# Rows of pairs 304 columns wide, and a drawn layout of weight places and product order for every five tiles

## The chip, the cores and the metric

The kernel runs on one core of one Trainium2 chip. What is compared is the device time of one execution in microseconds, as the median of several runs. Times of parts come from one profiled execution.

## The reference

Two layers of a bidirectional hybrid encoder over 16 meta tokens and 256 tokens (L = 272 rows, D = 2048), in float32. Per layer:

```
proj = h @ w_in                       # 2048 -> 6176 columns: GLA q, k, v, gate, decay, attention q, k, v
y    = [gla(q, k, v, gate, decay) | neighbourhood_attention(q, k, v)]
h    = layer_norm(alpha * h + y @ w_out)
h    = layer_norm(alpha * h + relu(h @ w_ff1)**2 @ w_ff2)     # 2048 -> 8192 -> 2048
```

The gated linear attention runs in both directions in chunks, the neighbourhood attention over a 4 x 64 grid with a relative bias. The meta rows are dropped from the output. Nearly all of the arithmetic is the four weight products.

## The kernel before

**Three products for one.** Each float32 operand is held as a high part rounded to float32r and a low part, the remainder. A product of a weight block w and an activation block x is the sum of high x high (`h`), high x low (`l`: the same weight block against the low activations) and low x high (`w`: the low weights against the high activations).

**Activations.** They lie transposed, 16 blocks of 128 features (32 for the MLP's inner layer, `y0` to `y15` and `u16` to `u31`). A block is a pair: one tile of shape 128 x 2 x PITCH, high row and low row beside each other (`pair`, L306). PITCH is 288 float32 columns, so the low row starts 288 columns after the high one, and one pair takes 2304 bytes of a partition. In the last layer the pairs of `y` and `u`, and the pairs of `x` after its first norm, are dense: their 256 + 256 columns follow each other with no gap (`Pair`, L45).

**Weights.** They come in tiles of 128 x 1024 (eight blocks of 128 x 128), 768 of them, 512 KB each, through SyncE's queue into `raw` (L189). ScalarE rounds a tile into `wh` (L212), VectorE subtracts to get `wl` (L213). `raw`, `wh` and `wl` have three buffers each, and `weights` (L175) makes each tile one ahead of the one in use. Where the eight blocks lie within a buffer of WIDE = 1280 columns is told by three numbers, the place of the first, the step from an even block to the odd one after it, and the step from pair to pair (`blocks`, L196, `HIGHS` and `LOWS`, L42 and L43). Most tiles of the first layer have the high blocks at (0, 128, 256), one run of 1024 columns, and the low ones at (0, 144, 320).

**Products by m.** `by_m` (L276) accumulates one output block of 128 features over all tiles of its weights in one PSUM bank. `eight` (L233) issues the products of a tile, in an order written as a string (`TURNS`, L44): `hlhlww` four times, 24 products of n columns, where n is 272 (layer one, and the parts of layer two that need the meta rows), 274 or 258 (two more columns carry the norm's gain and bias through the product, while the norm itself is still being computed) or 256. Where only the 256 tokens are needed (most of layer two), `once` is set: `hw` eight times, 16 products, in which `h` reads the high and the low row together, 512 columns, and `w` 256. In the attention part of layer two these 512 columns are read from a pair with a gap, as two runs of 256.

**Products by k.** `by_k` (L258) accumulates four (at the very start eight) output blocks at once, for the stages whose activations become ready one after another. Its order is its own (L273), in the same sense of `h`, `l` and `w`.

**Other work.** GLA, attention and norms are generators; `pump` (L125) advances them between tiles, so that their instructions stand in the queues of the engines between those of the products. TensorE does its part of them in between (L584 to L667 GLA, L723 to L789 attention, L910 the norms' means).

Of the kernel before, what the change touches and what calls it, by code (L numbers as in the profile page):

```python
# [2 lines left out]

# [11 lines left out]
P = 128  # L15
# [11 lines left out]
WB = 1024  # L27
# [9 lines left out]
WARM = 14  # L37
MEET = 2
PAD = 40
PITCH = 288  # L40
WIDE = 1280
HIGHS = {True: 24, False: 0}  # L42
LOWS = {True: (8, P + 32, 2 * P + 64), False: (0, P + 16, 2 * P + 64)}  # L43
TURNS = {True: "hwhwhwhwhwhwhwhw", False: "hlhlwwhlhlwwhlhlwwhlhlww"}  # L44


# [11 lines left out]
class Trunk:  # L58
    def __init__(self, ctx, tc, ins, out):
        self.ctx, self.tc, self.nc = ctx, tc, tc.nc  # L60
        self.i, self.out = ins, out
        self.bg, self.fg, self.credit, self.fcredit = deque(), deque(), 0, 0
        self.wants, self.due, self.late = {}, None, 0
        self.x = [None] * DC
        self.stream, self.ready = self.order(), deque()
        pool = lambda name, **k: ctx.enter_context(tc.tile_pool(name=name, **k))
        self.cp = pool("const", bufs=1)
        self.xp = pool("xhl", bufs=1)
        self.yp = pool("yhl", bufs=1)
        self.wp = pool("wst", bufs=3)  # L70
        self.jp = pool("jn", bufs=1)
        self.pm = pool("pm", bufs=4, space=PSUM)
        self.pb = pool("pb", bufs=4, space=PSUM)
# [80 lines left out]
    def order(self):  # L154

        i, first = self.i, [(), (WB // 2, WB)]
        for l in range(DEPTH):
            last = l + 1 == DEPTH
            na = [last and c % 3 == 0 for c in range(24)]
            groups = [(i["win"][l, g], [last and g in (3, 4, 5)] * 4 if g < 6 else na[4 * g - 24:4 * g - 20]) for g in range(12)]  # L160
            groups += [(i["wout"][l, g], [last and g > 0] * 4) for g in range(4)]
            for half in range(2):
                groups += [(i["wff1"][l, 8 * half + g], [last and (half > 0 or g > 2)] * 4) for g in range(8)]
                groups += [(i["wff2"][l, half, g], [last] * 4) for g in range(4)]
            if l == 0:
                for t in range(groups[0][0].shape[0]):
                    for w, _ in groups[:2]:
                        yield w[t], first.pop(0) if first else (WB,), False
                groups = groups[2:]
            for w, once in groups:  # L170
                n = w.shape[0]
                for t in range(n):
                    yield w[t], (WB,), once[4 * t // n]

    def weights(self):  # L175

        while len(self.ready) < 2:
            self.ready.append(self.made(*next(self.stream, (None, (), False))))
        return self.ready.popleft()

    def made(self, ap, ends, once):
        if ap is None:
            return None
        nc = self.nc
        raw = self.wp.tile([P, WB], F32, name="raw", tag="raw")
        wh, wl = (self.wp.tile([P, WIDE], F32R, name=nm, tag=nm) for nm in ("wh", "wl"))
        wh, wl = self.blocks(wh, HIGHS[once], P, 2 * P), self.blocks(wl, *LOWS[once])
        for c in map(slice, (0,) + ends, ends):
            nc.sync.dma_start(raw[:, c], ap[:, c])  # L189
            self.halves(raw[:, c], wh, wl, slice(c.start // P, c.stop // P))  # L190
        if not ends:
            self.head(ap, raw, wh, wl)
        return wh, wl
# [21 lines left out]
    def head(self, ap, raw, wh, wl):  # L215

        nc, q = self.nc, WB // 4
        both = self.xr.tile([P, 2, q + L], F32, name="head", tag="head", bufs=1)
        self.x[:2] = [self.pair(self.xp, "x", c) for c in range(2)]
        for c in range(2):  # L220
            nc.sync.dma_start(both[:, c], self.i["head"][:, c])
        nc.sync.dma_start(raw[:, 2 * q:], ap[:, 2 * q:])
        for c in range(2):
            at = slice(2 * c, 2 * c + 2)
            h, lo = (t[:, :L] for t in self.x[c])
            acts = lambda: self.split(both[:, c, q:], h, lo)
            weights = lambda: self.halves(both[:, c, :q], wh, wl, at)
            for f in (weights, acts) if c else (acts, weights):
                f()
        for at in (slice(4, 6), slice(6, 8)):  # L230
            self.halves(raw[:, at.start * P:at.stop * P], wh, wl, at)

    def eight(self, ps, wh, wl, x, n, first, last, once):  # L233

        mm = self.nc.tensor.matmul
        seen = dict.fromkeys("hlw", 0)
        for i, kind in enumerate(TURNS[once]):  # L240
            j = seen[kind]
            seen[kind] += 1
            w, v, o = wl if kind == "w" else wh, x[j], ps[:, :n]
            rhs = v[kind == "l"][:, :n]
            if once:
                rhs, o = (v.once, ps) if kind == "h" else (v[0][:, :T], ps[:, T:])
            mm(o, lhsT=self.block(w, j), rhs=rhs, start=first and not i, stop=last and i == len(TURNS[once]) - 1)  # L247

    def whole(self, parts):

# [53 lines left out]
    def pair(self, pool, name, c):  # L304
        both = pool.tile([P, 2, PITCH], F32R, name=f"{name}{c}", tag=f"{name}{c}", bufs=1)
        return Pair(both, dense=name in ("y", "u") and not self.full)  # L306
# [94 lines left out]
    def load_gates(self):  # L401

        place = lambda c: self.yp.tile([P, 2, PITCH], F32, name=f"gw{c}", tag=f"y{c}", bufs=1).rearrange("p a c -> p (a c)")[:, :512]
        *self.wup, self.wlr = (place(c) for c in (8, 9, 10))
# [563 lines left out]
    def reuse(self, name, c, dtype):  # L968

        t = self.xp.tile([P, 2, PITCH], dtype, name=f"{name}{c}", tag=f"x{c}", bufs=1)  # L970
        return t.rearrange("p a c -> p (a c)")[:, :512]
# [237 lines left out]
```

## Time and profile before

| | |
|---|---|
| median of 3 runs | 2337.14 us (2336.44 to 2337.54) |
| profiled execution | 2336.72 us, span of its instructions 2334.9 us |
| TensorE busy | 2326.3 us, 18180 matmuls |
| weight loads of TensorE busy | 2216.0 us |
| VectorE busy | 1527.4 us |
| ScalarE busy | 1211.8 us |
| granted TensorE clock, mean | 0.999 |
| read from HBM | 414.03 MB, 178 GB/s over the span |

Matmuls overlap each other in the records, and so do weight loads and matmuls: the duration of one matmul is longer than the distance between two starts. For the pace of a stage its length is divided by the number of its products.

### The profile page before, as it was taken

Reading aid. Unit: us, or ns where it says so; the run is one execution under the profiler, and the core shown is the slowest. Engines: PE = TensorE matmul, PEld = TensorE weight load, DVE = VectorE, ACT = ScalarE, POOL = GpSimd, SP = SyncE. Lnnn points to the kernel's source line nnn. Section 1 sums busy time; section 2 is a strip of 40 time slices with the busy share of each in tenths; the row PEclk is TensorE's granted clock in tenths of the full one; section 3 lists DMA queues with packets and bytes.
Section 4 is the critical chain, followed back from the end, with each engine's and each line's share of the span. In section 5 each row is a group of like instructions: output and inputs, shape, how many; then the busy total and the mean of one; then the engine's idle time right before and its main releaser. Section 6 shows DMA issues by size and latency. Waiting matters only on the chain.

```text
span 2334.9 us, 44618 instructions
## 1 busy us (share of the span) xinstructions
PE 2326.3 (100%) x18180; PEld 2216.0 (95%) x18180; DVE 1527.4 (65%) x2432; ACT 1211.8 (52%) x2100; POOL 129.4 (6%) x200
## 2 busy tenths in 40 slices
PE   9999999999999999999999999999999999999998
PEld 9999999999999999999999899989988888888888
DVE  5588777775544455546576887778766555666655
ACT  5666664564433344444456666655654334445443
POOL 0021110110000000000020111100100000000000
PEclk9999999999999999999999999999999999999999
DMA  8555545566666666665555555556666666667664
GB/s 264 154 163 154 152 140 178 173 179 181 179 182 178 180 179 181 181 181 177 178 183 168 172 163 158 162 158 189 191 191 193 193 190 191 193 193 221 190 191 151
DMA packets 118301, 419.02 MB, mean 179 GB/s; under 512 B 13512, under 2 KB 14024, under 8 KB 118096
## 3 DMA queue, kind: packets, MB, share of 16 engines
q1 hardware_dynamic: 117808, 415.65, 59.4%
q8 instruction: 142, 2.33, 0.4%
q14 instruction: 63, 0.52, 0.1%
q10 hardware_dynamic: 288, 0.52, 0.1%
HBM read 414.03 MB, written 2.10 MB: 178 GB/s over the span
## 4 chain that ended last, share of the span: by engine, by line
PE 98%; DVE 1%; issue 0%; ACT 0%; DVEq 0%; ACTq 0%
PE mm L247 86%; PE mm L273 6%; PE bg L273 1%; PE bg L784 1%; PE mm L723 1%; PE bg L584 1%; DVE wl L213 0%; PE bg L430 0%; PE mm L749 0%; DVE acc L1012 0%; PE mm L473 0%; PE bg L635 0%; PE bg L910 0%; PE bg L665 0%; PE bg L639 0%
## 5 line engine op out<-in xcount | busy, mean ns | idle before, releaser
L213 DVE TENSOR_TENSOR wl<-raw,wh 128x1024 fp32r<-128x1024 f32 (+1 forms) x770 | 942.9, 1225 | 637.8 <-ACT wh L212 631.8
L212 ACT CAST wh<-raw 128x1024 fp32r<-128x1024 f32 (+1 forms) x770 | 804.5, 1046 | 889.1 <-PE mm L247 703.0
L247 PE MATMUL mm<-x,wh 128*128 128x272 f32 (+3 forms) x5376 | 1094.3, 309 | 0.0
L247 PEld LDWEIGHTS mm<-x,wh 128*128 128x128 f32 x5376 | 803.7, 188 | 48.1 <-PE mm L723 0.6
L247 PE MATMUL mm<-x,wl 128*128 128x272 f32 (+3 forms) x3264 | 752.7, 283 | 0.0
L247 PEld LDWEIGHTS mm<-x,wl 128*128 128x128 f32 x3264 | 547.5, 188 | 0.0
L247 PE MATMUL mm<-y,wh 128*128 128x272 f32 (+2 forms) x2128 | 472.9, 319 | 0.0
L247 PEld LDWEIGHTS mm<-y,wh 128*128 128x128 f32 x2128 | 328.6, 188 | 26.9
L247 PE MATMUL mm<-u,wh 128*128 128x272 f32 (+2 forms) x1552 | 343.7, 318 | 0.0
L247 PE MATMUL mm<-y,wl 128*128 128x272 f32 (+1 forms) x1408 | 337.9, 282 | 0.7 <-DVE wl L213 0.7
L247 PEld LDWEIGHTS mm<-u,wh 128*128 128x128 f32 x1552 | 239.4, 188 | 19.5
L247 PE MATMUL mm<-u,wl 128*128 128x272 f32 (+1 forms) x1024 | 245.6, 282 | 0.0
L247 PEld LDWEIGHTS mm<-y,wl 128*128 128x128 f32 x1408 | 241.7, 188 | 1.4 <-DVE wl L213 1.1
L247 PEld LDWEIGHTS mm<-u,wl 128*128 128x128 f32 x1024 | 175.6, 188 | 0.0
L273 PE MATMUL mm<-x,wh 128*128 128x272 f32 (+1 forms) x512 | 83.8, 287 | 0.0
L273 PEld LDWEIGHTS mm<-x,wh 128*128 128x128 f32 x512 | 71.7, 191 | 0.0
L1000 POOL TENSOR_SCALAR acc<-acc,vec 128x272 f32<-128x272 f32 (+1 forms) x24 | 41.9, 1751 | 273.3 <-DVE acc L1012 155.3
L561 ACT COPY U<-S 128x272 f32<-128x272 f32 (+1 forms) x104 | 40.7, 429 | 23.2 <-DVE S L570 20.5
L273 PE MATMUL mm<-x,wl 128*128 128x272 f32 (+1 forms) x256 | 52.1, 286 | 0.5 <-DVE wl L213 0.5
L872 DVE TENSOR_TENSOR acc<-acc,mm 128x256 f32<-128x256 f32 (+1 forms) x71 | 30.3, 426 | 29.6 <-PE mm L247 29.1
L570 DVE TENSOR_TENSOR S<-S,dec 128x272 f32<-128x272 f32 (+1 forms) x112 | 46.3, 443 | 3.5 <-ACT U L561 2.5
L295 ACT CAST u<-ft 128x272 fp32r<-128x272 f32 (+1 forms) x64 | 26.2, 410 | 41.8 <-DVE ft L828 41.7
(265 smaller groups left out, 1647.5 us busy)
## 6 DMA issues: line engine op xcount, KB each, us to landing
raw<-in_wff SPq DMA_DIRECT2D x512, 512.0 KB, 3.8
raw<-in_win SPq DMA_DIRECT2D x190, 512.0 KB, 3.7
raw<-in_wout SPq DMA_DIRECT2D x64, 512.0 KB, 3.7
nb<-in_nab SPq DMA_DIRECT2D x16, 352.0 KB, 4.4
xraw<-in_xT SPq DMA_DIRECT2D x7, 272.0 KB, 5.9
out<-out SPq DMA_DIRECT2D x5, 256.0 KB, 3.1
brow<-in_norm SPq DMA_DIRECT2D x4, 256.0 KB, 4.5
gw<-in_wup SPq DMA_DIRECT2D x4, 196.0 KB
```

Source lines behind the costliest of these rows:

```text
L212: self.nc.scalar.copy(h, r)
L213: self.wl = self.nc.vector.tensor_tensor(lo, r, h.bitcast(F32), ALU.subtract).ins
L247: mm(o, lhsT=self.block(w, j), rhs=rhs, start=first and not i, stop=last and i == len(TURNS[once]) - 1)
L273: self.nc.tensor.matmul(ps[g + m][:, :n], lhsT=self.block(parts[p][0], 4 * j + m if first else 2 * m + j), rhs=acts[k + j][parts[p][1]][:, ...
L295: self.nc.scalar.copy(hi, src)
L561: nc.scalar.copy(U[:, lv % 4, j, :w].rearrange("p (n t h) -> p n t h", t=2, h=hb), bass.AP(S.tensor, S.offset + 2 * j * L, [S.ap[0], [2 * ...
L570: tt(o, o, totals(lv, odd, w), ALU.mult)
L584: nc.tensor.matmul(ps[b * 32:b * 32 + 32, o:o + w], lhsT=k[:, c:c + 32], rhs=q[:, r:r + w], start=True, stop=True)
L723: nc.tensor.matmul(ps[hh][:, t * NKEY:t * NKEY + NKEY], lhsT=q[hs, NM + t * P:NM + t * P + P], rhs=k[hs, t, :], start=True, stop=True)
L784: nc.tensor.matmul(po[t][hs, :P], lhsT=v2[ts, hs] if rest else v1[:, t, hs], rhs=p2[ts, hh, :] if rest else p1[:, 2 * hh + t, :], start=re ...
L872: tt(a, a, part, ALU.add)
L1000: nc.gpsimd.tensor_scalar(a, a, gain, bias, ALU.mult, ALU.add)
```

## The change

Two constants grow: PITCH from 288 to 304, so that a pair takes 2432 bytes and the low row starts 304 columns after the high one, and WIDE from 1280 to 1344 columns. A weight tile now has a kind instead of a flag:

- `once`: the dense short tiles, with places and order as before;
- `two`: the short tiles of layer two whose moving rows are read in two runs, with places of their own (before they had those of `once`);
- `all2` and `own2`: the tiles of 274 columns, and of 258, with places of their own (before: those of the tiles of 272);
- `all`: all else. Every five consecutive tiles of this kind draw, from a generator with a fixed seed, the first place and the step to the odd block for the high and for the low blocks (each 0 to 56 columns in steps of 8 beyond its least value; the step from pair to pair is 320 columns for both), and one of two orders of the 24 products, `hlhlww` four times or `hlw` eight times. The first two tiles of the program, which come in pieces, keep the old places. The order is used by `eight` only; `by_k` keeps its own. 86 layouts are drawn for 430 tiles: 376 by m of 272 columns, 38 by k of 272 and 16 by k of 256.

The same products are computed with the same weights; sums within a tile are added in another order where `hlw` is drawn.

```diff
-PITCH = 288
-WIDE = 1280
-HIGHS = {True: 24, False: 0}
-LOWS = {True: (8, P + 32, 2 * P + 64), False: (0, P + 16, 2 * P + 64)}
+PITCH = 304
+WIDE = 1344
+HIGHS = {"once": (24, P, 2 * P), "two": (0, P, 2 * P), "all": (0, P, 2 * P), "all2": (0, P, 2 * P), "own2": (0, P + 48, 2 * P + 64)}
+LOWS = {"once": (8, P + 32, 2 * P + 64), "two": (16, P + 16, 2 * P + 64), "all": (0, P + 16, 2 * P + 64),
+        "all2": (0, P + 48, 2 * P + 64), "own2": (0, P + 32, 2 * P + 64)}
+ORDERS = "hlhlwwhlhlwwhlhlwwhlhlww", "hlwhlwhlwhlwhlwhlwhlwhlw"
...
     def weights(self):
 
         while len(self.ready) < 2:
-            self.ready.append(self.made(*next(self.stream, (None, (), False))))
+            self.ready.append(self.made(*next(self.stream, (None, (), None))))
+        self.turn = self.turns.popleft()
         return self.ready.popleft()
 
-    def made(self, ap, ends, once):
+    def draw(self):
+
+        if self.drawn % 5 == 0:
+            r = lambda: 8 * self.dice.randrange(8)
+            self.places = (r(), P + r(), 2 * P + 64), (r(), P + r(), 2 * P + 64), ORDERS[self.dice.randrange(2)]
+        self.drawn += 1
+        return self.places
+
+    def made(self, ap, ends, kind):
...
-        wh, wl = self.blocks(wh, HIGHS[once], P, 2 * P), self.blocks(wl, *LOWS[once])
+        high, low, turn = self.draw() if kind == "all" and ends == (WB,) else (HIGHS[kind], LOWS[kind], TURNS[False])
+        self.turns.append(turn)
+        wh, wl = self.blocks(wh, *high), self.blocks(wl, *low)
...
-        for i, kind in enumerate(TURNS[once]):
+        turn = TURNS[True] if once else self.turn
+        for i, kind in enumerate(turn):
```

More of the change, by code (lines that the diff above doesn't have):

```diff
@@ L2 @@
 from contextlib import ExitStack
+from random import Random
 import concourse.bass as bass
@@ L64, in __init__ @@
         self.x = [None] * DC
-        self.stream, self.ready = self.order(), deque()
+        self.stream, self.ready, self.turns, self.drawn, self.dice = self.order(), deque(), deque(), 0, Random(5)
         pool = lambda name, **k: ctx.enter_context(tc.tile_pool(name=name, **k))
@@ L158, in order @@
             last = l + 1 == DEPTH
-            na = [last and c % 3 == 0 for c in range(24)]
-            groups = [(i["win"][l, g], [last and g in (3, 4, 5)] * 4 if g < 6 else na[4 * g - 24:4 * g - 20]) for g in range(12)]
-            groups += [(i["wout"][l, g], [last and g > 0] * 4) for g in range(4)]
+            kind = lambda short, name: name if last and short else "all"
+            na = [kind(c % 3 == 0, "two") for c in range(24)]
+            groups = [(i["win"][l, g], [kind(g in (3, 4, 5), "two")] * 4 if g < 6 else na[4 * g - 24:4 * g - 20]) for g in range(12)]
+            if last:
+                groups[0] = groups[0][0], ["all2"] * 4
+            groups += [(i["wout"][l, g], [kind(g > 0, "once")] * 4) for g in range(4)]
             for half in range(2):
-                groups += [(i["wff1"][l, 8 * half + g], [last and (half > 0 or g > 2)] * 4) for g in range(8)]
-                groups += [(i["wff2"][l, half, g], [last] * 4) for g in range(4)]
+                groups += [(i["wff1"][l, 8 * half + g], [kind(half > 0 or g > 2, "once") if half or g > 1 else ("all2", "own2")[last]] * 4)
+                           for g in range(8)]
+                groups += [(i["wff2"][l, half, g], [kind(True, "once")] * 4) for g in range(4)]
             if l == 0:
@@ L167, in order @@
                     for w, _ in groups[:2]:
-                        yield w[t], first.pop(0) if first else (WB,), False
+                        yield w[t], first.pop(0) if first else (WB,), "all"
                 groups = groups[2:]
-            for w, once in groups:
+            for w, kinds in groups:
                 n = w.shape[0]
                 for t in range(n):
-                    yield w[t], (WB,), once[4 * t // n]
+                    yield w[t], (WB,), kinds[4 * t // n]
     def weights(self):
         while len(self.ready) < 2:
-            self.ready.append(self.made(*next(self.stream, (None, (), False))))
+            self.ready.append(self.made(*next(self.stream, (None, (), None))))
+        self.turn = self.turns.popleft()
         return self.ready.popleft()
-    def made(self, ap, ends, once):
+    def draw(self):
[5 more added lines that the diff above has]
+    def made(self, ap, ends, kind):
         if ap is None:
+            self.turns.append(None)
             return None
@@ L246, in eight @@
                 rhs, o = (v.once, ps) if kind == "h" else (v[0][:, :T], ps[:, T:])
-            mm(o, lhsT=self.block(w, j), rhs=rhs, start=first and not i, stop=last and i == len(TURNS[once]) - 1)
+            mm(o, lhsT=self.block(w, j), rhs=rhs, start=first and not i, stop=last and i == len(turn) - 1)
     def whole(self, parts):
```

## The prediction

> **What bounds the kernel now.** I read the page first (parts 1, 2 and 4), then the waits of TensorE, then TensorE's groups by shape, then windows cut to single stages, and last the timeline of a few tiles.
>
> ```profile
> span 2334.9 us, 44618 instructions
> PE 2326.3 (100%) x18180; PEld 2216.0 (95%) x18180; DVE 1527.4 (65%) x2432; ACT 1211.8 (52%) x2100; POOL 129.4 (6%) x200
> PEclk9999999999999999999999999999999999999999
> ...
> PE 98%; DVE 1%; issue 0%; ACT 0%; DVEq 0%; ACTq 0%
> ```
> ```profile
> PE mm L247 <- DVE wl L213: 0.7, 1, 0.7
> PE mm L273 <- DVE wl L213: 0.5, 1, 0.5
> ```
>
> TensorE is busy for 2326.3 of 2334.9 us, at full clock in every slice, the chain that ends last is 98% TensorE, and its products by m and by k wait 1.2 us in all for weights. So neither loads nor splits set the time. What sets it is how many ns apart the products start. A busy matmul row does not show that, since one of 286 ns overlaps the next; a stage's length divided by its products does. The groups by shape give the counts:
>
> ```profile
> L247 PE MATMUL mm<-x,wh 128*128 128x272 f32 x3584 | 588.5, 286 | 0.0
> L247 PE MATMUL mm<-x,wh 128*128 128x512 f32 x1152 | 400.2, 392 | 0.0
> L247 PE MATMUL mm<-x,wl 128*128 128x272 f32 x1792 | 364.9, 285 | 0.0
> L247 PE MATMUL mm<-x,wl 128*128 128x256 f32 x1152 | 321.8, 279 | 0.0
> L247 PE MATMUL mm<-y,wh 128*128 128x272 f32 x1408 | 229.9, 285 | 0.0
> L247 PE MATMUL mm<-u,wh 128*128 128x272 f32 x1024 | 167.0, 285 | 0.0
> L247 PE MATMUL mm<-y,wl 128*128 128x272 f32 x704 | 143.2, 285 | 0.0
> L247 PE MATMUL mm<-u,wl 128*128 128x272 f32 x512 | 104.2, 284 | 0.0
> ```
>
> Products by m of 272 columns: 3584+1792+1408+1024+704+512 = 9024, which is 376 tiles of 24. From 512 against 256 columns a column costs (392-279)/256 = 0.44 ns. The windows hold whole stages and show products by m alone (length, TensorE busy, number):
>
> ```profile
> 445.50:488.06 42.56, 42.55 (x336) 1.00 0.57 173
> 1620.18:1660.87 40.69, 40.68 (x336) 1.00 0.59 181
> 816.64:1004.37 187.73, 187.73 (x1538) 1.00 0.62 180
> ...
> 1284.64:1307.40 22.76, 22.75 (x128) 1.00 0.64 189
> 1969.39:2145.18 175.79, 175.79 (x1026) 1.00 0.65 192
> ```
> and the products by k of 256 columns:
> ```profile
> 1660.87:1683.70 22.83, 22.83 (x192) 1.00 0.63 186
> ```
>
> They are, in order: tiles of 274 columns, of 258 columns, 64 tiles of 272 columns (1536 products; two more hang over from before), eight short tiles (512 and 256 by turns) whose pair is read in two runs, and 64 short tiles whose pair is dense (1024 products). Starts are 42.56/336 = 126.7, 40.69/336 = 121.1, 187.73/1536 = 122.2, 22.76/128 = 177.8 and 175.79/1024 = 171.7 ns apart, and 22.83/192 = 118.9 by k. In all six TensorE never stops, yet the width doesn't explain them. Brought to 272 columns at 0.44 ns each, 274 gives 125.8, 258 gives 127.3, and 256 gives 126.0: all slower than the 272 itself, whose weights lie at the same places. The two kinds of short tile have the same weights at the same places and the same columns, and differ by 6.1 ns a product only in how the moving rows lie. So the distance between starts depends on how the two reads of a product meet, and 272 columns over rows of 288 meet them well.
>
> The timeline where a stage of 272 columns begins (first start of each six products; line engine group) shows it within one set of addresses:
>
> ```profile
> 488.06 0.66 PE L273 MATMUL mm<-x,wh 128*128 128x272 f32 x4
> ...
> 488.81 0.67 PE L273 MATMUL mm<-x,wh 128*128 128x272 f32 x4
> ...
> 489.57 0.66 PE L273 MATMUL mm<-x,wh 128*128 128x272 f32 x4
> ...
> 490.31 0.65 PE L273 MATMUL mm<-x,wh 128*128 128x272 f32 x4
> ...
> 491.04 0.65 PE L273 MATMUL mm<-x,wh 128*128 128x272 f32 x4
> ```
>
> Three sixes take 2.25 us (125.0 ns a product), then 0.73 a six (122): the stream opens slow and settles into a faster beat. A layout whose beat is no better than the opening would stay at 125.
>
> **The change, part by part.** No matmul, DMA, cast or split is added or taken away; addresses and, in about half of the tiles, the order within a tile change.
>
> *Drawn layouts.* They reach the 376 tiles by m of 272 columns, 38 of 40 tiles by k of that width, and 16 tiles by k of 256: 430 tiles, 86 draws. Each draw moves four starts by 0 to 56 columns in steps of 8, and picks `hlhlww` or `hlw`. Before shows one layout, so I bound the mean of 86 by the nearest rows: below by 122.2, the settled beat, above by 127.3. The five values at 272 columns (127.3, 126.0, 125.8, 125.0, 122.2) have a mean of 125.3; I take 125.2, that is +3.0 ns, and 124.0 to 126.4 for the mean of many draws. There are 9024 + 38x24 = 9936 such products: 9936 x 3.0 = +29.8 us, all on the path, since TensorE has no idle time to give. What is already unsettled can't be lost again: an opening costs 2.25 - 3x0.733 = 0.05 us, and with some fifty openings (an estimate: sixteen head pairs and eight GLA heads, each cutting in two or three times) that is 2.5 us to take off. +27.3. The 256-wide tiles by k are at 126.0 for 272 already: 0.
>
> *Fixed places of the 274s, the 258s and the two-run tiles.* 24 tiles of 274 (576 products), 16 of 258 (384) and 40 short tiles read in two runs (640) get places of their own. If all reached the best beat of their width (274 at 122.2+0.9, 258 at 122.2-6.2, two runs at the dense 171.7) they gave back 576x3.6 + 384x5.1 + 640x6.1 = 2.1+2.0+3.9 = 8.0 us; if none, 0. I take half, -4.0.
>
> *Rows of 304.* Dense pairs keep their places for the weights, but a pair takes 2432 bytes instead of 2304, so in steps of 256 bytes (the 64 columns that the draws span) every second pair now starts half a step off. The some 250 dense tiles, by the code about 4000 products, stand at 171.7; the two-run row 177.8 is the other end, and below them I see room for little, as 343.4 ns for 768 columns is 0.447 a column, the lowest here. I take +0.2 ns, +0.8 us, and -1 to +3 ns for the range.
>
> *Casts and splits.* The high part, one run of 1024 for most tiles, is written in eight runs of 128; the low part is so already.
>
> ```profile
> L213 DVE TENSOR_TENSOR wl<-raw,wh 128x1024 fp32r<-128x1024 f32 x766 | 940.7, 1229 | 636.7 <-ACT wh L212 630.8 <-PE mm L247 0.7 <-PE bg L910 0.5
> L212 ACT CAST wh<-raw 128x1024 fp32r<-128x1024 f32 x766 | 802.6, 1048 | 887.9 <-PE mm L247 703.0 <-issue 91.2 <-PE mm L273 35.8
> ```
> ```profile
> 300.00:500.00 200.00, 160.19 (x314) 1.00 0.55 164
> ```
>
> A tile lasts 24x122.2 ns = 2.93 us and its cast and split 1.05+1.23 us on two engines, made a tile ahead, and both wait for TensorE (703.0 us) and for each other (630.8). `hlw` asks for the low part two products, 0.25 us, earlier. VectorE is fullest at 300 to 500 us (last row), 80%. That cover hides it: 0, and 1 us in the range. The scheduler shifts some dozens of small instructions of the GLA stage on VectorE and ScalarE: 0, at 1 us either way.
>
> Sum: 27.3 - 4.0 + 0.8 = +24.1 on the profiled execution's 2336.72 us (1.8 over its span), 2360.8; the median of the runs stands 0.4 above that execution, so 2361.
>
> A rule of the Trainium skill speaks against all of this. "TensorE: Matmul & The Clock Gate", Step-by-step, says that the array reads moving rows and weights over two independent ports, and that "Loading the next tile's weights doesn't steal SBUF read bandwidth from the running matmul." By it no place would matter and the drawn tiles would cost 0; the trace disagrees, with 171.7 and 177.8 ns for the same widths and weights and 125.0 and 122 at the same addresses, though it can't say whether weights or the moving rows' own start is at fault.
>
> **The rivals.**
>
> *Places don't matter (no effect).* The beat might belong to the width alone (272 is 17 times 16, the other two are not). For it: one width settles everywhere at 122.2, whatever the buffer. Against: the two short kinds, and 256, a rounder number, at 126.0. Then 9936 x 0 and no fixed kind gains: 2337.
>
> *The draws are better than the places before (faster).* If rows of 304 bring a better beat to most layouts, every drawn product and the fixed kinds gain. It turns at a mean of 122.5 ns (0.3 ns x 9936 = the 3 us that the fixed kinds give). Price: at the lowest cost per column seen, 0.447x272 = 121.6 ns, it is -0.6x9936 = -6.0 and -8.0: 2323. Against it: all 86 draws would have to beat the best layout that the trace shows. By the skill's figure for an undisturbed stream (same page, "Back-to-back issue gap": N/2.4 + 2.5 ns) 272 columns would take 115.8 as an estimate, and this rival would reach 2337 - 9936x6.4/1000 = 2273; no row here comes near that.
>
> *The dense short tiles lose their beat too (slower still).* Half way to the two-run row is +3 ns on 4000 products: +12 us, 2373. For it: their moving rows shift and their weights don't. Against: in a dense tile the low blocks already lie at two different places (8 and 168 columns) against rows of one, and the pace is still the best per column here.
>
> *Weights come late.* If the eight-run write took ScalarE and VectorE a third longer (0.35 and 0.4 us), the crowded 300 to 500 us would need 160 + 68x0.4 = 187 of 200 us and the chain would pass to VectorE in places: +5 us, 2366. Against: the low part is written in eight runs already, and its 1229 ns is VectorE's cost of two inputs.
>
> **How the numbers follow.** Forecast 0.70, dense tiles 0.12, late weights 0.06, no effect 0.05, faster 0.07. The forecast's own ends: mean 124.0 gives 9936x1.8 = 17.9 - 2.5 - 8.0 = +7.4, less 2 for dense and scheduling, 2342; mean 126.4 gives 41.7 - 2.5 + 3 = +42, 2379. That range takes in the two slower rivals; nine tenths of the forecast and of these make about 0.79. About 0.2%, 4.7 us, is what a measurement of this kernel can tell from no change: faster 0.07, same 0.05 (no effect; a forecast so low is left out), slower 0.88.
>
> **What would show it.** Right: TensorE still near 100% with no new waits; in the windows of the 272-column stages the starts 124 to 126.5 ns apart, changing from one group of five tiles to the next, some groups below 122.2 and some at 128 or more; 274 and 258 no slower than 126.7 and 121.1; dense tiles at 171 to 172.5. Wrong: groups of five all alike (places don't matter), a mean of 122.5 or less, a dense stage at 174, or TensorE waiting on the split for more than some us.

## The result

The changed kernel takes 2377.48 us (median of 4 runs, 2376.56 to 2377.57), the kernel before 2337.07 (2336.44 to 2337.54, 4 runs): a ratio of 1.0173, 95% interval 1.0162 to 1.0185, or +40.4 us. The forecast was 2361.0 with a range of 2342 to 2379. The sign is right and the time lies near the upper end of the range; the surplus of 16 us comes mainly from one step of the working, and in part from a second; both are named below.

The page of the profiled execution after (2377.42 us), lines of its parts 1, 2 and 4, and then TensorE's waits for weights (us in total, times, longest):

```profile
span 2375.7 us, 44615 instructions
PE 2366.1 (100%) x18180; PEld 2245.4 (95%) x18180; DVE 1528.4 (64%) x2432; ACT 1212.8 (51%) x2100; POOL 130.4 (5%) x200
...
PEclk9999999999999999999999999999999999999999
...
PE 96%; DVE 2%; issue 1%; ACT 0%; DMA 0%; POOL 0%; SPq 0%; DVEq 0%; ACTq 0%; POOLq 0%
```
```profile
PE mm L267 <- DVE wl L232: 0.5, 1, 0.5
PE mm L293 <- ACT wh L231: 0.4, 1, 0.4
PE mm L293 <- DVE wl L232: 0.4, 1, 0.4
```

The same 18180 matmuls at the same clock keep TensorE busy for 39.8 us more, and they wait for weights no more than before (1.3 us against 1.2). Nearly all of the loss is pace, the distance from one product's start to the next. The windows of two whole stages of after (length, TensorE busy, number; TensorE alone), and within the first one three stretches of five tiles each:

```profile
816.64:1004.37 187.73, 187.73 (x1501) 1.00 0.57 175
838.66:853.59 14.93, 14.93 (x123) 1.00 0.55 177
853.59:868.53 14.94, 14.94 (x123) 1.00 0.53 177
868.53:883.73 15.20, 15.20 (x122) 1.00 0.54 174
1969.39:2145.18 175.79, 175.79 (x1006) 1.00 0.61 188
```

The numbers hold two or three products that hang over from before the window. In the 187.73 us in which 1536 products of 272 columns started before, 1499 start now: 125.2 ns instead of 122.2. Five tiles are 120 products: 14.93, 14.94 and 15.20 us are 124.4, 124.5 and 126.7 ns, so the pace changes from draw to draw (that is, from one drawn layout to the next), but little. In the dense stage 1004 products start where there were 1024: 175.1 ns instead of 171.7.

From the start-to-start distances of all products of both traces, by kind (the mean leaves out distances in which TensorE paused or did other work; the last column is the difference of the full sums; "by m" and "by k" are the two ways of issuing a tile):

| kind (products) | before, ns | after, ns | us |
|---|---|---|---|
| 272 columns by m (9024) | 122.44 | 125.23 | +24.9 |
| 272 by k (960) | 122.64 | 125.24 | +2.1 |
| 256 by k (384) | 118.89 | 117.31 | -0.5 |
| 274 (576) | 126.70 | 128.02 | +0.8 |
| 258 (384) | 121.08 | 120.09 | -0.4 |
| two runs, 512 and 256 (320 each) | 235.69, 117.42 | 232.30, 117.14 | -0.3 |
| dense, 512 (2016) | 226.82 | 232.54 | +11.3 |
| dense, 256 (2016) | 116.69 | 118.03 | +2.6 |
| all other TensorE work | | | 0.1 |

The sum is +40.6. Two kinds carry it: the tiles of 272, whose loss was forecast, and the dense short tiles, whose loss was not.

### The profile page after: what moved, and what is told of

Same layout as the page of the kernel before. It is cut to its first block, busy times and chain, and to the rows that moved or that the text cites. A ratio compares the mean times of both kernels' runs of the same rounds, so it can differ in the third digit from the quotient of the medians.

```text
span 2375.7 us, 44615 instructions
## 1 busy us (share of the span) xinstructions
PE 2366.1 (100%) x18180; PEld 2245.4 (95%) x18180; DVE 1528.4 (64%) x2432; ACT 1212.8 (51%) x2100; POOL 130.4 (5%) x200
## 4 chain that ended last, share of the span: by engine, by line
PE 96%; DVE 2%; issue 1%; ACT 0%; DMA 0%; POOL 0%; SPq 0%; DVEq 0%; ACTq 0%; POOLq 0%
PE mm L267 85%; PE mm L293 6%; PE bg L293 1%; PE bg L804 1%; DVE wl L232 1%; PE mm L743 1%; PE bg L604 0%; DMA raw<-in_win 0%; PE bg L450 0%; PE mm L769 0%; DVE acc L1032 0%; ACT wh L231 0%; PE mm L493 0%; PE bg L930 0%; PE bg L655 0%
## 5 line engine op out<-in xcount | busy, mean ns | idle before, releaser
L267 PE MATMUL mm<-x,wh 128*128 128x272 f32 (+3 forms) x5376 | 1158.4, 311 | 0.0
L267 PEld LDWEIGHTS mm<-x,wh 128*128 128x128 f32 x5376 | 846.7, 188 | 51.4 <-PE mm L743 0.6
L267 PE MATMUL mm<-x,wl 128*128 128x272 f32 (+3 forms) x3264 | 850.5, 285 | 0.0
L267 PEld LDWEIGHTS mm<-x,wl 128*128 128x128 f32 x3264 | 583.5, 188 | 0.0
L267 PE MATMUL mm<-y,wh 128*128 128x272 f32 (+2 forms) x2128 | 496.7, 323 | 0.0
L267 PEld LDWEIGHTS mm<-y,wh 128*128 128x128 f32 x2128 | 342.0, 188 | 31.0
L267 PE MATMUL mm<-y,wl 128*128 128x272 f32 (+1 forms) x1408 | 366.1, 284 | 0.5 <-DVE wl L232 0.5
L267 PE MATMUL mm<-u,wh 128*128 128x272 f32 (+2 forms) x1552 | 360.0, 322 | 0.0
L267 PE MATMUL mm<-u,wl 128*128 128x272 f32 (+1 forms) x1024 | 265.7, 284 | 0.0
L267 PEld LDWEIGHTS mm<-y,wl 128*128 128x128 f32 x1408 | 252.0, 188 | 1.3 <-DVE wl L232 0.9
L293 PEld LDWEIGHTS mm<-x,wh 128*128 128x128 f32 x512 | 71.4, 188 | 0.8 <-ACT wh L231 0.6
```

The lines of the kernel that those rows point to most:

```text
L293: self.nc.tensor.matmul(ps[g + m][:, :n], lhsT=self.block(parts[p][0], 4 * j + m if first else 2 * m + j), rhs=acts[k + j][parts[p][1]][:, ...
```

## The experiments

Each is compared with the kernel before on the same chip (2335.6 to 2336.9 us in all of them). Where a ratio is given, the kernel ran four times or more; a time without one is a single run. The repeated kernels spread over 0.4 to 2.2 us. Diffs are shortened, and "..." stands for lines left out. Paces are means over a kind's products as in the table; windows show the same two stretches of time as above, the first in products of 272 columns, the second in dense ones.

### Each half of the change alone

Is it the places of the weights, the rows, or how the two lie to each other? First the draws over rows of 288 (an edit of the changed kernel), then the old places over rows of 304 (an edit of the kernel before):

```diff
-PITCH = 304
+PITCH = 288
```

> The changed kernel with rows of 288 columns again; the draws and the places of the three other kinds stay. Theory A (the drawn places cost the tiles of 272 columns their beat, the wider rows cost only the dense short tiles): 272 columns stay at about 125.2 ns a product (+27 us), the dense short tiles return from 232.5 and 118.0 to 226.8 and 116.7 ns (-14 us), in all about 2363 us. Theory B (the distance from row to row alone sets the beat, the places of the weights are nothing): 272 columns return to 122.4 ns whatever the draw, in all about 2337 us. Theory C (both must fit): as A here; the fixed places with rows of 304 tell C from A.

```diff
-PITCH = 288
+PITCH = 304
```

> The kernel before with rows of 304 columns and nothing else. Theory A (the draws cost the tiles of 272 columns): 272 columns near 122.4 ns, dense short tiles at 232.5 and 118.0, about 2337 + 14 = 2351 us. Theory B (row width alone): 272 columns at 125.2, about 2377 us. Theory C (weights and rows must fit each other, and almost any pairing but the one found for 288 is a common one): 272 columns at 124.4 to 126.7, as one of the draws, about 2370 to 2391 us.

The draws alone: 2364.01 us, ratio 1.0115 (1.0099 to 1.0132). Its two windows:

```profile
816.64:1004.37 187.73, 187.73 (x1501) 1.00 0.59 175
1969.39:2145.18 175.79, 175.79 (x1026) 1.00 0.66 192
```

The rows alone: 2381.49 us, ratio 1.0190 (1.0175 to 1.0205):

```profile
816.64:1004.37 187.73, 187.73 (x1498) 1.00 0.59 175
1969.39:2145.18 175.79, 175.79 (x1006) 1.00 0.65 188
```

Over rows of 288 the draws cost the 272s their beat (125.42 ns by m) and leave the dense tiles where they were (1024 products): +27.3 us. The old weight places over rows of 304 cost the 272s as much (125.47), and cost the dense tiles too (232.77 and 118.32 ns, +15.0 us). So neither the weights' places nor the rows decide alone: each edit breaks the beat of the 272s, and the second then has nothing left to break (both: 125.23). The dense loss comes with the rows alone.

### Draws for the dense tiles

```diff
-high, low, turn = self.draw() if kind == "all" and ends == (WB,) else (HIGHS[kind], LOWS[kind], TURNS[False])
+high, low, turn = self.draw() if kind == "once" else (HIGHS[kind], LOWS[kind], TURNS[False])
```

Once over rows of 304 and once over rows of 288:

> The changed kernel with rows of 304 in which the dense short tiles draw their places, five tiles at a time, and all others keep fixed places (the tiles of 272 columns those of the kernel before). If the places of the weights decide how dense tiles run over rows of 304, groups of five differ by more than 1% and some come near the 343.4 ns for a pair of products of 512 and 256 columns that rows of 288 gave; if the rows alone decide, all groups stay at about 350.5 ns. The 272s as in the run of the kernel before with rows of 304.

> Rows of 288 columns; the dense short tiles draw their places, five tiles at a time, all others have fixed places (the 272s those of the kernel before, the three other kinds their own). If the dense tiles of the kernel before have a narrow fit too, nearly every group leaves 343.5 ns for a pair of products of 512 and 256 columns and goes to 346 to 356, as the draws did over rows of 304 (mean 350.1): about 2334 + 2016 x 6 ns = 2346 us. If for dense tiles rows of 288 alone are enough, all groups stay at 343.5 and the whole at 2334 us.

The tiles of 272 have the old places in both (and are slow over rows of 304, 125.5 ns). The times are 2378.77 and 2345.92 us. The dense stage of the one and of the other:

```profile
1969.39:2145.18 175.79, 175.79 (x1008) 1.00 0.64 189
```
```profile
1969.39:2145.18 175.79, 175.79 (x1009) 1.00 0.62 189
```

Over rows of 288, 51 drawn layouts take 349.7 ns for a pair of products of 512 and 256 columns on average, against 343.5 at the old places; one (first places at 16, odd steps 56 beyond the least, high and low) reaches 343.5, and the worst takes 353.4. Over rows of 304 the mean is 350.0 and the best 347.7. So the dense tiles had a good layout too, and a rare one (one draw of 51 found another), and over rows of 304 none was drawn.

### One place at a time

In the kernel with draws over rows of 288, a list `SCAN` takes the place of the draws. Most groups of five tiles have the old layout, and each of the others differs from it in one thing (the groups with a longer step to the odd high block also have the longer step from pair to pair, which by itself cost nothing):

```diff
-self.places = (r(), P + r(), 2 * P + 64), (r(), P + r(), 2 * P + 64), ORDERS[self.dice.randrange(2)]
...
+self.places = SCAN.get(self.drawn // 5, (HIGHS["all"], LOWS["all"], ORDERS[0]))
```

> Rows of 288 columns, the places of the changed kernel for the three other kinds, and in the place of the draws a list: the layout of the kernel before for most tiles of 272 columns, and between them groups of five in which one thing differs from it: first high place 8 to 56 columns on, high step 8 to 56 longer, first low place 8 to 56 on, low step 0 to 56 instead of 16, high and low moved together by 8, 16 or 32, pair step of the high blocks 320 for 256, low blocks in one run, order hlw. If the fit is narrow (each shift breaks it), every group but the base is at 124.3 to 127.8 ns a product, as the draws, and the base at 122.2. If only the high blocks must meet the rows, the groups with other low places stay near 122.2. If the order matters, hlw at the base's places leaves 122.2; in the draws the two orders had the same mean. Moving both together tells weights against rows (125) from weights against weights (122.2).

2347.41 us. Windows of five tiles each, in order: first high block 8 columns on; the old layout, with its opening; step from pair to pair of the high blocks 320 instead of 256; odd high block 16 columns on, with that step; first low block 8 on; first low block 40 on; order `hlw`:

```profile
514.49:529.55 15.06, 15.06 (x122) 1.00 0.57 175
604.89:619.61 14.72, 14.72 (x122) 1.00 0.60 179
634.56:649.29 14.73, 14.73 (x122) 1.00 0.58 179
664.25:679.38 15.13, 15.13 (x122) 1.00 0.57 174
769.42:784.49 15.07, 15.07 (x123) 1.00 0.60 176
844.04:858.91 14.87, 14.87 (x122) 1.00 0.58 177
1009.16:1024.36 15.20, 15.20 (x122) 1.00 0.59 174
```

Divided by 120 these are 125.5, 122.7, 122.8, 126.1, 125.6, 123.9 and 126.7 ns. All groups in which something was moved by 8 to 56 columns lie at 123.9 to 126.7, the least move of 8 included; high and low moved together by 8, 16 or 32 lose it too (124.6, 125.5, 124.6), so it isn't only the high weights against the low. The one thing that cost nothing was a step longer by 64 columns, 256 bytes. And the order, which made no difference among the draws of the changed kernel (125.2 for both), costs as much as a wrong place when the places are right.

The paces are not spread evenly. The last four tiles of the groups with the longer step, with the low block 40 on and with `hlw`:

```profile
637.56:649.29 11.73, 11.73 (x98) 1.00 0.57 180
847.02:858.91 11.89, 11.89 (x98) 1.00 0.58 178
1012.20:1024.36 12.16, 12.16 (x98) 1.00 0.59 174
```

A tile of 24 products that has settled lasts 2933, 2973 and 3040 ns here, and by the starts in the trace nearly every other group of the scan settles at one of these or at 2987, 3000, 3013 or 3027 ns: 220 and 223 to 228 times 13.33 ns. A settled dense tile of the last stage fits the same step: 2747 ns before (206 times), 2800 after (210). So a layout that doesn't fit loses some whole steps of 13.3 ns in a tile, three to eight in the scan. What a step is, no run shows.

### The low row's distance from the high one

Over the kernel before, the low row 280 columns after the high one; and then, with `LOW = 288` and `PITCH = 304`, pairs 2432 bytes apart but the low row where it was:

```diff
+LOW = 280
...
-parts = (flat[:, :T], flat[:, T:2 * T]) if dense else (both[:, 0, :], both[:, 1, :])
+parts = (flat[:, :T], flat[:, T:2 * T]) if dense else (flat[:, :LOW], flat[:, LOW:LOW + 274])
...
```

> The kernel before with the low row starting 280 columns after the high one instead of 288, pairs still 2304 bytes apart; dense pairs as before. If the fit needs the low row where it was, the 272s go to about 125.4 ns (+27 us, 2364); if it is the distance from pair to pair alone, they stay at 122.4 (2337). Dense short tiles stay at 226.8 and 116.7 in both.

> The kernel before with pairs 2432 bytes apart as in the changed one, but the low row starting 288 columns after the high one as before. If the distance from pair to pair decides, 272s at about 125.5 and dense at 232.8 and 118.3, about 2381 us as with rows of 304 in full; if the distance from high to low row decides, 272s back at 122.4 and only the dense tiles slow, about 2352.

2364.82 and 2384.71 us. The first:

```profile
816.64:1004.37 187.73, 187.73 (x1497) 1.00 0.58 175
1969.39:2145.18 175.79, 175.79 (x1027) 1.00 0.65 192
```
and the second:
```profile
816.64:1004.37 187.73, 187.73 (x1493) 1.00 0.59 175
1969.39:2145.18 175.79, 175.79 (x1006) 1.00 0.64 188
```

The 272s take 125.6 and 125.9 ns. Eight columns between high and low row are enough to lose the beat, and 288 between them isn't enough to keep it when the pairs stand 2432 bytes apart. Both distances count.

### Rows moved, then rows and weights moved together

The rows of all pairs with a gap 8 columns on; and then the weights of the 272s 8 columns on as well:

```diff
+START = 8
...
-parts = (flat[:, :T], flat[:, T:2 * T]) if dense else (both[:, 0, :], both[:, 1, :])
+parts = (flat[:, :T], flat[:, T:2 * T]) if dense else (both[:, 0, START:], both[:, 1, START:])
...
```
```diff
-HIGHS = {True: 24, False: 0}
-LOWS = {True: (8, P + 32, 2 * P + 64), False: (0, P + 16, 2 * P + 64)}
+HIGHS = {True: 24, False: START}
+LOWS = {True: (8, P + 32, 2 * P + 64), False: (START, P + 16, 2 * P + 64)}
```

> The kernel before with the moving rows of every pair with a gap 8 columns (32 bytes) further on, weights as before; the distances from pair to pair and from high to low row stay. If only the places of weights and rows against each other count, this must cost what moving the weights against the rows did (124 to 126 ns a product of 272 columns, +18 to +38 us: 2355 to 2375). If the rows' pitch alone counted, it would stay at 122.2 ns and 2337. The two-run tiles move against their weights too, by at most 4 us either way; dense tiles stay at 343.5 ns for their pair of products.

> The same 8 columns, and both weight blocks of the 272-column tiles 8 columns further on as well. If places count only against each other, everything is back: 122.2 to 122.5 ns and 2337, give or take 3 for the two-run tiles. If weights and rows each need a place of their own in memory, the two losses stay (moving both weight blocks by 8 alone gave 124.6 ns): 124.6 ns or more and at least 2357.

2363.09 and 2335.91 us, against 2336.27 before. Rows alone:

```profile
816.64:1004.37 187.73, 187.73 (x1504) 1.00 0.59 175
```
and rows and weights:
```profile
816.64:1004.37 187.73, 187.73 (x1538) 1.00 0.60 180
```

High and low weights 8 on cost (124.6 ns in the scan), the rows 8 on cost (125.0 ns), and both 8 on cost nothing: 1536 products to the window, as before. What counts is where weights and rows lie to each other.

### Rows of 304 with the fit restored, in two ways

With rows of 304 every second pair starts 32 columns off, counted modulo 64 columns. In the first kernel the odd weight blocks follow them (with the edits of the low row 288 after the high one):

```diff
-HIGHS = {True: 24, False: 0}
-LOWS = {True: (8, P + 32, 2 * P + 64), False: (0, P + 16, 2 * P + 64)}
+HIGHS = {True: (24, P + 32, 2 * P + 64), False: (0, P + 32, 2 * P + 64)}
+LOWS = {True: (8, P, 2 * P + 64), False: (0, P + 48, 2 * P + 64)}
...
```

> Rows of pairs 304 wide, the low row again 288 columns after the high one (that alone took 2384.71 us), and now the odd weight blocks moved by 32 columns more, so that they step half of 64 columns from pair to pair as the rows do: against the rows every weight block lies where it lay before, modulo 64 columns, except where a tile's first pair is one of the eight (y0 to y7) that start half a step off, and in some tiles by k. If only the places against each other count, modulo 64 columns: products by m of 272 columns back to 122.2 to 122.6 ns against x, u and y8 to y15, the 64 dense tiles of the last stage at 343.5 ns a pair again, and 44 tiles against y0 to y7 slow, at 124.5 to 126.5 ns; in sum 1056 x 3.3 + some 480 by k x 3 + 344 dense pairs x 7 = 3.5 + 1.4 + 2.4 = +7.3 us, 2341 to 2346. If rows of 304 are slow by themselves, or what is between high and low weights counts, it stays above 2370.

That failed: 2380.33 us, ratio 1.0187 (1.0170 to 1.0204). The 272s stay slow, and fewer dense products start than with the rows alone (995 against 1004).

```profile
816.64:1004.37 187.73, 187.73 (x1504) 1.00 0.59 176
1969.39:2145.18 175.79, 175.79 (x997) 1.00 0.63 186
```

The second kernel leaves the weights as they were and starts the odd pairs 32 columns into their rows (2432 + 128 bytes are ten times 256):

```diff
+LOW = 288
...
-flat = both.rearrange("p a c -> p (a c)")
+flat = both.rearrange("p a c -> p (a c)")[:, start:start + 2 * LOW]
...
-return Pair(both, dense=name in ("y", "u") and not self.full)
+return Pair(both, dense=name in ("y", "u") and not self.full, start=c % 2 * 32)
```

> Rows of pairs 304 wide, weights placed as before, the low row 288 columns after the high one, and the odd pairs start 32 columns into their rows, so that all pairs start at the same place modulo 64 columns, as before. Product by product the distance from rows to weights, modulo 64 columns, is that of fit304, which stayed slow at 2380.33 us; what differs is that here the rows of one product also lie against the weights of the next products as before. If the whole sequence of places counts (the weights of the next product are loaded while the rows of this one pass), the settled beat is back: 122.2 to 122.6 ns against x, u and y8 to y15, 343.5 ns a pair in the dense last stage, with the 44 tiles of 272 against y0 to y7, which lie 32 columns off as a whole, at 124.5 to 126.5, and dense ones too: 2341 to 2346. If rows spaced 304 apart are slow by themselves (a period longer than 64 columns), it stays at 2375 to 2385.

2343.28 us, ratio 1.0028 (1.0018 to 1.0037):

```profile
816.64:1004.37 187.73, 187.73 (x1538) 1.00 0.60 180
1969.39:2145.18 175.79, 175.79 (x1025) 1.00 0.65 192
```

Both beats are back over rows of 304: 1536 products of 272 columns and 1023 dense ones start in their windows. Within the same run the tiles against `y0` to `y7`, whose pairs by the order in which the code makes them lie 32 columns off as a whole, are the ones that stay slow: 124.85 ns by m (44 tiles, none under 124.67; 122.26 before), against 122.46 for all other tiles of 272. The dense tiles against the same pairs take 350.9 ns for a pair of products (343.8 before). 44 tiles of 24 products at 2.6 ns are 2.7 us and 43 dense tiles of 8 pairs at 7.2 ns are 2.5, most of the +6.4. The tiles against `y8` to `y15`, which come right behind them and have the right places, lose a little too: 0.45 ns a product and 2.2 a pair, 1.2 us.

The two kernels have the same distances, modulo 64 columns, from the rows of each product to its own weights. They differ in how the rows and weights of a product lie to the rows and weights of its neighbours in the order, and by 2.6 ns a product (125.04 against 122.46, apart from `y0` to `y7`). So a product's own distance doesn't decide alone; the sequence counts. That fits the scan, in which the order mattered. That it is the weights of the next product, loaded while the rows pass, is the nearest reading, but it was only argued: no run moves the next weights and leaves all else.

### The own places of the three fixed kinds

The changed kernel over rows of 288, without draws: the kernel before, plus new places for the 274s, the 258s and the tiles read in two runs.

```diff
-high, low, turn = self.draw() if kind == "all" and ends == (WB,) else (HIGHS[kind], LOWS[kind], TURNS[False])
+high, low, turn = HIGHS[kind], LOWS[kind], TURNS[False]
```

> The kernel before with the three kinds' own places of the changed kernel and nothing else (rows of 288, no draws). From the run with rows of 288 and draws: 274s 126.70 to 126.13 (0.3 us), 258s 121.08 to 118.91 (0.8 us), two-run tiles 235.69 to 232.05 and 117.42 to 115.47 (1.8 us), in all -2.9 us: about 2334 us, 0.9988 of before. If what the three kinds gain is lost again in the tiles next to them, no change.

2334.13 us (11 runs), ratio 0.9989 (0.9980 to 0.9998): -2.6 us, the one version measurably ahead of both kernels, though by less than the 0.2% that the prediction took as its bound. 258 columns take 118.91 ns (before 121.08), 274 take 126.08 (126.70), two runs 232.00 and 115.46 (235.69 and 117.42): 0.8 + 0.4 + 1.8 = 3.0 us by the paces.

## Why the prediction was right, and where it was wrong

**The time: inside the range, with two misses in the same direction.** The range reached up to 2379 because it was drawn to take in the slower rivals. What happened is the forecast and one of these rivals together: the dense tiles lost their beat, and a dense stage at 174 ns, set down as a sign of being wrong, came as 175.1.

**Drawn layouts, forecast +27.3: right.** Measured +24.9 + 2.1 = 27.0. Both estimates held: a lost beat stays near the pace of an opening (125.0), and the openings, already slow, can't lose again (122.44 on average before against the settled 122.2, 0.24 x 9984 = 2.4 us; forecast 2.5). The mean itself, forecast 125.2 and found 125.2, is in part luck: it came from five values between 122.2 and 127.3, four of them from openings and other widths. Tiles by k of 256 columns, forecast 0, gained 0.5.

**Their spread: wrong.** "Some groups below 122.2 and some at 128 or more" did not come. Of the 83 draws that reached tiles of 272 columns all but one lie at 124.4 to 126.7 ns; the other is at 124.1, and its undisturbed tiles by k at 123.35. The bounds, 122.2 from the one layout before and 127.3 from products of 258 columns, were too wide: the fit is narrow, none of these draws met it, and outside it they cost some 2 to 4 ns a product. The rival that the draws are better had no ground in the 272s. The last draw, for tiles by k of 256 columns, did better than before (115.6 ns against 118.9), so for that width the kernel before did not have the best pattern.

**Rows of 304 for the dense tiles, forecast +0.8, at most +3 ns a product: the step that failed.** Measured +11.3 + 2.6 = +13.9 us, 343.5 to 350.6 ns for two products, 3.5 a product. It is 13.1 us beyond its forecast and the fixed places below are 4.1; against that, the drawn tiles and the tiles by k of 256 came out 0.8 lower. Together this is the surplus of some 16 us. The prediction saw that every second pair would start half a step off, gave the loss as a rival with 0.12 at +12 us, and argued against it that the low blocks lie at two places against rows of one and are fast all the same. That argument mistook a fit to a pattern of two places for indifference: over rows of 288, 50 of 51 drawn layouts of the dense tiles are slower than the old one. The rows-only kernel shows this term by itself (+15.0 us), and the kernel with odd pairs started 32 columns on takes it back. The profile before had a hint of it: the two-run and the dense tiles, with the same weights, differ only in their rows.

**Fixed places, forecast -4.0: nearly nothing.** Measured +0.8 - 0.4 - 0.3 = +0.1. Over rows of 288 these places do give 2.6 us; over rows of 304 the 274s lose what the 258s and the two-run tiles gain. The windows of after, products by m alone, for the 274s and the 258s:

```profile
453.05:496.13 43.08, 43.02 (x336) 1.00 0.56 171
1648.50:1688.90 40.40, 40.20 (x335) 1.00 0.60 182
```

43.02/336 is 128.0, where "no slower than 126.7" was forecast; 40.20/335 is 120.0, better than 121.1 as forecast. The step judged places without the rows that they were to fit.

**Casts, splits and late weights, forecast 0: right.** VectorE's and ScalarE's groups of after:

```profile
L232 DVE TENSOR_TENSOR wl<-raw,wh 128x1024 fp32r<-128x1024 f32 x766 | 940.1, 1228 | 671.8 <-ACT wh L231 656.5 <-PE bg L804 5.3 <-PE mm L267 1.6
L231 ACT CAST wh<-raw 128x1024 fp32r<-128x1024 f32 x766 | 802.1, 1048 | 927.6 <-PE mm L267 690.3 <-issue 148.7 <-PE mm L293 37.4
```

1228 and 1048 ns, within 1 ns of before: writing the high part in eight runs costs nothing that these rows show, and the rival of late weights falls.

**Places don't matter: wrong, as the prediction held.** Moving eight columns costs 26.8 us and moving the other side after them gives it back. The rule of the Trainium skill's "TensorE: Matmul & The Clock Gate", Step-by-step, that a weight load takes no read bandwidth from the running matmul, would have left the place without effect, and the traces disagree: 125.0 and 122.2 ns for the same products, weights and bytes, by addresses alone.

## What to carry to other kernels

When TensorE never waits, divide a stage's length by its products: a duration in the records (286 ns before, 288 now) hides a pace of 122 or 125. Where that pace is best, treat weight places, row pitch, high-to-low distance and order of products as one pattern; a change to one of them has to be priced for every kind of tile that shares it. Here the pattern could be moved as a whole for nothing (2335.91 us against 2336.27), and if a pitch must change, moving the rows' starts so that all of them stand alike modulo 64 float32 columns kept it for all tiles but those against `y0` to `y7`.

## What the runs showed of the hardware

Four things were not expected. The fit is narrow: 8 columns (32 bytes) off cost as much as larger shifts, some 2 to 4 ns of 122. The loss comes in steps: settled tiles of the scan and of the dense last stage last whole multiples of 13.3 ns. The fit repeated after 64 columns, 256 bytes, in the two places where this was tried (the scan's longer step, and odd pairs started at ten times 256 bytes instead of nine), and it was lost at nine and a half times 256 bytes. And it belongs to the sequence of products, not to one alone: the kernel whose odd weight blocks followed the rows kept the own distances, modulo 64 columns, and stayed at 125.04 ns. What in the chip repeats after 256 bytes, and whether it is a neighbour's weights that collide with the rows, stays open.
